# Moving the conditions of extra blocks ahead of the transposes, an earlier first expert, and an on-chip last sum, in a mixture-of-experts block

## The chip, the cores and the metric

The kernel runs on one core of a Trainium2 chip. The metric is the device time of one execution in microseconds (us), as the median of several runs. A difference under 1% (about 15 us here) can't be told from no change by a measurement of this kernel.

## The reference

The kernel computes one decoder block for 512 tokens of width 1024: an adaLN-modulated mixer (a state-space branch and a gated-MLP branch), then a top-4-of-32 mixture of experts, then a final norm. Almost all of the time goes into the experts:

```python
logits = (tok @ router_w + router_b)
top_val, top_idx = lax.top_k(logits, 4)
weights = softmax(top_val)
# for every expert e, on the rows that chose it:
gu = xb @ w_in[e] + b_in[e]             # 1024 -> 2048
gate, up = gu[:, :1024], gu[:, 1024:]
gate = jnp.minimum(gate, 7.0); up = jnp.clip(up, -7.0, 7.0)
act = (up + 1) * (gate * sigmoid(1.702 * gate))
y = act @ w_out[e] + b_out[e]           # 1024 -> 1024
out = out.at[row_tok].add(y * row_w)
# then
x = x + gate2 * out
return rms_norm(x, final_g)
```

All 32 experts are used, with float32 weights: 12 MB for each expert, 384 MB in all.

## The kernel before

The first 394 us compute the mixer, the router and the tables that say which token sits in which slot of which expert. Then come the 32 experts, one after the other, and at about 1508 us the final norm.

**Rows of an expert.** Each expert has a main block of 64 slots ("ab"). Its rows are gathered into `xab` by an indirect DMA that gpsimd issues, and the weights stream past them. An expert with more rows has extra blocks: a `single` (32 slots, "c") or a `pair` (64 slots), each inside a run-time condition `tc.If(single[e] > 0)` or `tc.If(pair[e] > 0)`. With the inputs of the runs shown, 15 of the 32 experts have one: twelve a single (experts 4, 6, 9, 12, 13, 16, 18, 22, 25, 27, 28, 30) and six a pair (11, 12, 17, 22, 26, 27). The other 17 are called plain below. The branch that skips a body on TensorE waits until the engine has finished what it has in hand.

**Weights.** `weight_loads` streams, for each expert, eight `wi` tiles and four `wo` tiles of 1 MB each through one pool of 19 buffers. SyncE (SP) issues the loads in order, in program order with its own copies of the conditions; a load can go out only when the readers of the buffer that it takes have let go of it. `prefetch(12 * (e + 3))` stands at the end of each expert.

**TensorE's order** is written out by hand (`manual_schedule`), as the code stands. For one expert: the two extra-block "up" products (`c_up`, and `ab_up` on the pair) inside their conditions; the main `ab_up` (64 matmuls in the trace's count, where each fp32 matmul instruction shows as two), with `before_last` called before its last four: it computes `swiglu` of the first half, transposes it (`act` to `aab`) and starts the second product with its biases. Then the conditions of the extra "down" products (`c_down`, pair `ab_out`); then the first half of the main "down" product (`ab_down`, 16), `halfway` (the second half's transposes, the next expert's row transposes `rows_of` and bias matmuls `main_sums`), and the second half (16). `give` scatters the result into the DRAM tensor `acc` by an indirect DMA with addition.

**The final norm** loads `acc` into four `fin` tiles of 128 x 1024, squares and sums on ScalarE, computes the inverse root by short VectorE steps (`final_rsqrt`), multiplies and stores. Two of the four tiles are multiplied by `final_g` on gpsimd.

**VectorE, ScalarE and gpsimd** are ordered by the framework's scheduler inside the experts, and by hand in the final norm.

## Time and profile before

| what | value |
|---|---|
| median of three runs | 1538.41 us (1537.32 to 1547.82) |
| profiled execution | 1535.88 us, span 1534.0 us |
| mean granted TensorE clock | 0.966 of full speed |
| TensorE matmul busy | 1392.9 us (91% of the span) |
| VectorE, ScalarE, gpsimd busy | 30%, 23%, 12% |
| DMA | 497.13 MB, mean 324 GB/s |

TensorE is busy most of the time and DMA is close to full in long stretches, so an average can't say which of the two sets the pace; each stretch has to be read by itself. The sum of busy time counts stretched matmuls too: TensorE at half its clock is busy twice as long.

### The profile page before, as it was taken

The page shows a single profiled execution, that of the slowest core. Times are in us where ns is not written, and L with a number is a line of the kernel's source. Part 1 is how long each engine was busy: PE and PEld are TensorE (multiplying, and loading weights), DVE is VectorE, ACT ScalarE, POOL GpSimd, SP SyncE. Part 2 cuts the span into 40 slices and gives each one's busy share as a digit, 9 for nine tenths or more (in the row PEclk, how much of TensorE's full clock was granted, in tenths as well). Part 3 has the DMA queues.
Part 4 walks back from the last instruction along what each step waited for, and adds up shares of the span by engine and source line. Part 5 has one row for each costly group of instructions (what it writes and reads, how often), then busy time and mean ns, then how long its engine had stood idle before and what let it go on. Part 6 is the DMA issues. An engine that isn't in the chain of part 4 may idle for free. (4 is left out here: it accounts for less than half of the span.)

```text
span 1534.0 us, 22365 instructions
## 1 busy us (share of the span) xinstructions
PE 1392.9 (91%) x7925; PEld 674.5 (44%) x7926; DVE 453.6 (30%) x1121; ACT 350.1 (23%) x841; POOL 187.1 (12%) x158
## 2 busy tenths in 40 slices
PE   5987999999699899979999999999999999999992
PEld 3766877787433233323333333333333333333330
DVE  7685842575421121111111211111112111121113
ACT  3453232334211111111120111111121121202112
POOL 3113000000201010201010110111101111101001
PEclk9998999999599999989999999999999999999997
DMA  9703687394799999999997899999999999769953
GB/s 312 205 14 120 195 290 237 117 388 149 290 399 400 410 405 409 404 401 404 410 402 276 326 399 407 407 354 397 406 403 384 391 411 406 296 231 356 403 215 132
DMA packets 128919, 497.13 MB, mean 324 GB/s; under 512 B 23588, under 2 KB 31236, under 8 KB 95972
## 3 DMA queue, kind: packets, MB, share of 16 engines
q1 hardware_dynamic: 113844, 468.50, 77.9%
q0 software_dynamic: 11888, 20.84, 5.9%
q10 hardware_dynamic: 3008, 5.38, 1.0%
q8 instruction: 116, 1.90, 0.5%
q14 instruction: 63, 0.52, 0.1%
HBM read 476.75 MB, written 20.40 MB: 324 GB/s over the span
## 5 line engine op out<-in xcount | busy, mean ns | idle before, releaser
L1313 PE MATMUL pu<-wi,xab 128*64 128x512 f32 x2048 | 458.7, 600 | 16.3 <-PEq L1432 13.5
L1313 PEld LDWEIGHTS pu<-wi,xab 128*64 128x64 f32 x2048 | 163.9, 138 | 288.2 <-issue 282.2
L1326 PE MATMUL pd<-wo,aab 128*64 128x512 f32 x1024 | 235.7, 602 | 22.5 <-PEq L1455 20.8
L1288 ACT ACTIVATE s<-g 128x256 f32<-128x256 f32 x88 | 36.7, 417 | 671.7 <-DVE g L1287 656.4
L1326 PEld LDWEIGHTS pd<-wo,aab 128*64 128x64 f32 x1024 | 74.1, 138 | 162.9 <-issue 148.9
L1287 DVE TENSOR_SCALAR g<-pu 128x256 f32<-128x256 f32 x64 | 27.0, 421 | 323.9 <-PE pu L1313 323.3
L1347 PE MATMUL pc<-wi,xc 128*32 128x512 f32 x768 | 88.4, 606 | 13.7 <-DMA wi<-in_moe_w_in 10.9
L1279 ACT ACTIVATE xab<-pt,sh2c,g2c 128x64 f32<-128x64 f32 x304 | 94.1, 415 | 11.4 <-PE pt L1273 9.7
L1313 PE MATMUL pc<-wi,xab 128*64 128x512 f32 x384 | 83.7, 594 | 1.2 <-ACT xab L1279 1.1
L1335 DVE SCALAR_TENSOR_TENSOR yab<-pd,tab,gate2h 128x512 f32<-128x512 f32 x32 | 24.0, 750 | 201.2 <-PE pd L1326 201.2
L1250 POOL DMA_INDIRECT xab<-hrow,tab x32 | 34.1, 1064 | 315.7 <-PE pt L1273 312.8
L1364 POOL DMA_INDIRECT acc<-yab,tab x32 | 51.0, 1594 | 151.8 <-DVE yab L1335 66.4
L386 PE MATMUL g<-hlo,whi 128*128 128x512 f32 x160 | 65.5, 410 | 2.8 <-DVE hlo L492 2.8
L386 PE MATMUL g<-hhi,whi 128*128 128x512 f32 x160 | 66.1, 413 | 1.7 <-ACT hhi L498 1.7
L386 PE MATMUL g<-hhi,wlo 128*128 128x512 f32 x160 | 64.7, 404 | 0.0
L1364 POOL DMA_INDIRECT acc<-yc,tab x12 | 19.9, 1656 | 361.4 <-DVEq L1455 242.2
L1287 DVE TENSOR_SCALAR g<-pc 128x256 f32<-128x256 f32 x24 | 10.2, 425 | 174.7 <-PE pc L1347 100.6
L174 ACT ACTIVATE whi<-wraw 128x1024 fp32r<-128x1024 f32 x46 | 47.4, 1054 | 57.5 <-PE g L386 36.0
L1281 ACT ACTIVATE aab<-pt 128x256 f32<-128x256 f32 x64 | 24.6, 384 | 150.3 <-PE pt L1273 150.3
L1347 PEld LDWEIGHTS pc<-wi,xc 128*32 128x32 f32 x768 | 23.3, 110 | 69.7 <-issue 52.4
L175 DVE TENSOR_TENSOR wlo<-wraw,whi 128x1024 fp32r<-128x1024 f32 x36 | 43.1, 1219 | 33.2 <-ACT whi L174 32.9
L1313 PEld LDWEIGHTS pc<-wi,xab 128*64 128x64 f32 x384 | 27.1, 137 | 55.2 <-issue 49.6
(446 smaller groups left out, 1589.2 us busy)
## 6 DMA issues: line engine op xcount, KB each, us to landing
wi<-in_moe_w_in SPq DMA_DIRECT2D x256, 1024.0 KB, 18.1
wo<-in_moe_w_out SPq DMA_DIRECT2D x128, 1024.0 KB, 19.8
adaw<-in_ada_w SPq DMA_DIRECT2D x16, 1024.0 KB, 8.3
wraw<-in_w_in SPq DMA_DIRECT2D x12, 1024.0 KB, 5.0
wraw<-in_ada_w SPq DMA_DIRECT2D x8, 1024.0 KB, 9.0
wraw<-in_w_out SPq DMA_DIRECT2D x4, 1024.0 KB, 4.9
xt<-in_x SPq DMA_DIRECT2D x4, 512.0 KB, 5.3
wraw<-in_w_in SPq DMA_DIRECT2D x4, 512.0 KB, 12.6
```

What stands on the lines that cost most here:

```text
L174: sc.activation(dst_hi, src, AF.Copy)
L175: lo.tensor_sub(dst_lo, src, dst_hi)
L386: pe.matmul(P["ps"][m], l, r, start=(k == 0 and n == 0), stop=(k == 2 * P["n"] - 1 and n == 2))
L1250: gp.indirect_dma_start(out=dst, out_offset=None, in_=rows_, in_offset=bass.IndirectOffsetOnAxis(ap=idx, axis=0), bounds_check=n * S - 1, ...
L1279: sc.activation(t[:, o:o + w], ps[:, o:o + w], AF.Identity, scale=g2c[:, k:k + 1], bias=sh2c[:, k:k + 1])
L1281: sc.activation(t, ps[:, 0:128 * n], AF.Copy)
L1287: v.tensor_scalar(g, p[:, 0:256], LIMIT, None, op0=OP.min)
L1288: sc.activation(sg, g, AF.Sigmoid, scale=ALPHA)
L1313: pe.matmul(p[u][64 * g:64 * g + 64, :].rearrange("p (a b) -> p a b", a=2), xT[:, k % 4, 64 * (k // 4):64 * (k // 4) + 64], wi[k][:, :, 51 ...
L1326: pe.matmul(p[64 * g:64 * g + 64, :], aT[:, k % 2, 16 * (k - k % 4):16 * (k - k % 4) + 64], wo[k // 2 + j][:, k % 2, 512 * g:512 * g + 512 ...
L1347: pe.matmul(p[32 * g:32 * g + 32, :].rearrange("p (a b) -> p a b", a=2), xT[:, k % 2, 32 * (k // 2):32 * (k // 2) + 32], wi[k][:, :, 256 * ...
L1364: gp.indirect_dma_start(out=rows_, out_offset=bass.IndirectOffsetOnAxis(ap=icol, axis=0), in_=y, in_offset=None, compute_op=OP.add)
```

## The change

Four edits, in the one diff:

1. The conditions move. `c_down` and the pair's "down" now stand in `before_last`, in front of the transposes of the first half. `c_up` and the pair's "up" become `extra_up`, and `halfway` of expert e calls `extra_up(e + 1)`, in front of the transposes of the second half: they run before the second half of expert e's own "down" product, and no condition with a body is left between two experts.
2. The first expert's "up" product begins early: half of its steps, `UP[:8]`, run before and behind the table matmuls, ahead of the condition `most > 6`.
3. The last expert's rows are not scattered to `acc`. `last_places` builds a one-hot matrix `hot` on VectorE, eight matmuls `ys` put the rows in token order, and VectorE adds them to `fin`, which is loaded from `acc` while the last expert still runs.
4. The final norm is written anew: three VectorE steps for each tile (two adds, one multiply by both factors), two inverse roots of two tiles each, and no gpsimd.

```diff
+    def sums(t, n, tile_):
+        r = tile_("slt")
+        sc.activation(r[0:n], t[0:n, 0:96], AF.Copy)
+        return r
+
+    def tables(r, n, reps, tab, mul, o, ps_, tile_):
...
+    UP = [(k, u) for k in range(4) for u in range(2)] + [(k, u) for u in range(2) for k in range(4, 8)]
+
+    def ab_up(xT, wi, p, between=None, steps_=UP):
+
+        for k, u in steps_:
             if between and (k, u) == (7, 1):
                 between()
...
-    def ab_out(pd, aT0, aT1, wo, row):
+    def ab_out(pd, aT0, aT1, wo, row, kept=False):
+
 
         ab_down(pd, aT0, 0, wo, (0, 1, 4, 5))
         aT1 = aT1()
         ab_down(pd, aT1, 1, wo, (0, 1, 4, 5))
         y = mo.tile([128, 512], F32, tag="yab", bufs=2, name="yab")
         v.scalar_tensor_tensor(y, pd, row[:, 2:3].bitcast(F32), gate2h, op0=OP.mult, op1=OP.mult)
+        if kept:
+            return y
         give(y, acc2, row[:, 1:2])
...
-    def later_tables(ch):
+    def later_sums(ch):
 
         t = PT()
         if ch > 1:
             later_hots(ch)
         for i in range(4):
             spread(t, 128, i)
-        s_ = rows_of(0) if ch == 1 else None
+        return sums(t, 128, mo_tile)
+
+    def later_tables(ch, r):
         tab = mo.tile([128, 512], F32, tag="yab", bufs=2, name="tl")[:, 0:384].bitcast(I32) if ch > 1 else None
         tab = tab.rearrange("p (n e w) -> p n e w", n=4, w=3) if ch > 1 else tab1
-        tables(t, 128, rep32, tab, 4.0, 0, PT, mo_tile)
+        tables(r, 128, rep32, tab, 4.0, 0, PT, mo_tile)
         if ch == 1:
-            tables(t, 64, rep64, tabp, 2.0, 2, PT, mo_tile)
+            tables(r, 64, rep64, tabp, 2.0, 2, PT, mo_tile)
             v.copy_predicated(tab1[:, 0], pair4.unsqueeze(2).to_broadcast([128, 32, 3]), tab1[:, 2])
         gp.dma_start(tabl[4 * ch - 2:4 * ch + 2].rearrange("n p f -> p n f"), tab.rearrange("p n e w -> p n (e w)"))
-        return s_
+
+    fin, places = [], {}
+
+    def load_fin():
+        for i in range(4):
+            nc.sync.dma_start(fin[i][:, 0], acc[128 * i:128 * i + 128])
+
+    def last_places(e):
+
+        hot = xab[(e + 1) % 3]
+        t = pos[:, 0:5]
+        v.tensor_copy(t[:, 4:5], tab0[:, 0, e, 1:2])
+        v.tensor_sub(t[:, 4:5], t[:, 4:5], offs[:, 2:3])
+        for i in range(4):
+            v.tensor_scalar(t[:, i:i + 1], t[:, 4:5], 0.5, -1.0 - 128.0 * i, op0=OP.mult, op1=OP.add)
+            v.tensor_scalar(hot[:, 128 * i:128 * i + 128], iota_l, t[:, i:i + 1], None, op0=OP.is_equal)
+        places["hot"] = hot
 
...
-    xT0 = later_tables(1)
+    slots1 = later_sums(1)
     sel0 = selectors(0)
+    p0 = main_sums(0, sel0)
+    xT0 = rows_of(0)
+    ab_up(xT0, W[0][0], p0, None, UP[:4])
+    later_tables(1, slots1)
+    ab_up(xT0, W[0][0], p0, None, UP[4:8])
     most = nc.values_load(nbt[0:1, 96:97], min_val=0, max_val=NBMAX)
     with tc.If(most > 6):
         for ch in (2, 3, 4):
-            later_tables(ch)
+            later_tables(ch, later_sums(ch))
         spaced(PT(), sel0, 62)
...
+    def extra_up(e, sel):
+
+        (wi, _), n, x_, last = W[e], e // 16, xce[e % 3], acts(3, "actc")
         with tc.If(single[e] > 0):
             c_up(transposed(x_[:, 512:768], 2, "xc", 2, True), wi, sel, n, last[2])
         with tc.If(pair[e] > 0):
@@ -1435,32 +1461,48 @@
             ab_up(xp, wi, up_biases(sel, n, pp))
             for t, a_ in zip(pp, last):
                 swiglu(t, a_)
+        return last
+
+    def expert(e, xT, sel, p, more=None):
+        (wi, wo), n = W[e], e // 16
+        x_ = xce[e % 3]
+        if e + 2 < NE:
+            gather_first(e + 2)
+            gather_more(e + 2)
+        sel1 = selectors(e + 1) if e + 1 < NE else None
+        act = acts(2, "act")
+        last = extra_up(0, sel) if e == 0 else more
         aT, nxt = [], []
 
         def before_last():
             swiglu(p[0], act[0])
+            with tc.If(single[e] > 0):
+                c_down(transposed(last[2], 2, "ac", 2), wo, sel, n, tab1[:, 0, e])
+            with tc.If(pair[e] > 0):
+                lT = [transposed(t, 2, "ac", 2) for t in last[0:2]]
+                ab_out(out_biases(spaced(PC(), sel, 5), sel, n), lT[0], lambda: lT[1], wo, tabp[:, 0, e])
             aT.append(transposed(act[0], 2, "aab", 2))
             aT.append(out_biases(pab.tile([128, 512], F32, tag="pd", name="pd"), sel, n))
 
         def halfway():
+            more_ = extra_up(e + 1, sel1) if sel1 is not None else None
             aT1 = transposed(act[1], 2, "aab", 2)
             if sel1 is not None:
-                nxt.extend((rows_of(e + 1), sel1, main_sums(e + 1, sel1)))
+                nxt.extend((rows_of(e + 1), sel1, main_sums(e + 1, sel1), more_))
             return aT1
 
-        ab_up(xT, wi, p, before_last)
+        ab_up(xT, wi, p, before_last, UP if e else UP[8:])
         swiglu(p[1], act[1])
-        with tc.If(single[e] > 0):
-            c_down(transposed(last[2], 2, "ac", 2), wo, sel, n, tab1[:, 0, e])
-        with tc.If(pair[e] > 0):
-            lT = [transposed(t, 2, "ac", 2) for t in last[0:2]]
-            ab_out(out_biases(spaced(PC(), sel, 5), sel, n), lT[0], lambda: lT[1], wo, tabp[:, 0, e])
-        ab_out(aT[1], aT[0], halfway, wo, tab0[:, 0, e])
+        if e == NE - 1:
+            last_places(e)
+            fin.extend(H([128, 2, 1024], name="fin") for _ in range(4))
+            load_fin()
+        places["y"] = ab_out(aT[1], aT[0], halfway, wo, tab0[:, 0, e], e == NE - 1)
         if e + 2 < NE:
             prefetch(12 * (e + 3))
         return nxt
 
-    s_ = xT0, sel0, main_sums(0, sel0)
+    s_ = xT0, sel0, p0
...
+        load_fin()
+
+    ys = []
+    for i in range(4):
+        ys.append([PC(), PC()] if i % 2 else [pab.tile([128, 512], F32, tag=f"pu{u}", name="ys") for u in range(2)])
+        for g in range(2):
+            pe.matmul(ys[i][g], places["hot"][64 * g:64 * g + 64, 128 * i:128 * i + 128],
+                      places["y"][64 * g:64 * g + 64], start=True, stop=True)
...
+    def final_add(i):
+        for g in range(2):
+            o = fin[i][:, 0, 512 * g:512 * g + 512]
+            v.tensor_add(o, ys[i][g], o)
+
+    def final_out(i):
+        v.scalar_tensor_tensor(fin[i][:, 1], fin[i][:, 0], fr[:, i:i + 1], fg, op0=OP.mult, op1=OP.mult)
 
     def final_store(i):
         nc.sync.dma_start(dap(out, i * 128 * 1024, [[1024, 128], [1, 1024]]), fin[i][:, 1])
 
+    r01, r23 = [final_rsqrt(slice(a, a + 2)) for a in (0, 2)]
+    for i in range(3):
+        final_add(i)
+        final_square(i)
+    for _ in r01:
+        pass
+    final_add(3)
+    final_square(3)
     for i in range(4):
-        final_square(i)
-    final_mul(0)
-    r0, r1_, r2 = [final_rsqrt(slice(a, b)) for a, b in ((0, 1), (1, 2), (2, 4))]
-    final_mul(2, gp)
-    final_mul(3, gp)
-    for _ in zip(range(4), r0):
-        pass
-    final_mul(1)
-    in_turn(chain(r0, (final_out(0, lo, lo + 256) for lo in range(0, 1024, 256))), r1_)
-    final_store(0)
-    final_out(1, eng=sc)
-    final_store(1)
-    for _ in r2:
-        pass
-    for i in (2, 3):
-        final_out(i, 0, 640)
-        final_out(i, 640, 1024, sc)
+        if i == 2:
+            for _ in r23:
+                pass
+        final_out(i)
         final_store(i)
```

On TensorE, around the first expert's start, from the slot sums (`pt<-rx,oh`) on; `slt,reps` are the table matmuls. Before:

```order
L1121 MATMUL pt<-rx,oh 128x96 x16
L1273 MATMUL pt<-ident,xab_3352 128x128 x4
L1201 MATMUL pt<-slt,reps 128x96 x5
L1410 TENSOR_LOAD nbt
L1411 COMPARE_AND_BRANCH
```

After:

```order
L1121 MATMUL pt<-rx,oh 128x96 x16
L1299 MATMUL pu<-bhl,sel 128x512 x2
L1276 MATMUL pt<-ident,xab_3352 128x128 x4
L1318 MATMUL pu<-wi,xab 64x512 x8
L1204 MATMUL pt<-slt,reps 128x96 x5
L1318 MATMUL pu<-wi,xab 64x512 x8
L1441 TENSOR_LOAD nbt
L1442 COMPARE_AND_BRANCH
```

The bias matmuls and half of the first expert's "up" product (`pu<-wi,xab`, 16 of 30 rows) now stand in front of the condition at `most > 6` (L1411 before, L1442 after), with the table matmuls between them.

On TensorE, from the first half of an expert's "down" product (`pd<-wo,aab`) to the conditions of the next expert's extra blocks. `xce` holds the extra blocks' rows, `pc` their sums. Before:

```order
L1326 MATMUL pd<-wo,aab 64x512 x8
L1273 MATMUL pt<-ident,act 128x128 x2
L1273 MATMUL pt<-ident,xab_3353 128x128 x4
L1296 MATMUL pu<-bhl,sel 128x512 x2
L1326 MATMUL pd<-wo,aab 64x512 x8
L1257 TENSOR_LOAD nbt x2
L1263 COMPARE_AND_BRANCH
L1263 UNCONDITIONAL_BRANCH x2
L1265 COMPARE_AND_BRANCH
L1265 UNCONDITIONAL_BRANCH x2
L1430 COMPARE_AND_BRANCH
L1273 MATMUL pt<-ident,xce_3356 128x128 x2
```

After, from the same first half on:

```order
L1331 MATMUL pd<-wo,aab 64x512 x8
L1456 COMPARE_AND_BRANCH
L1276 MATMUL pt<-ident,xce_3356 128x128 x2
L1299 MATMUL pc<-bhl,sel 128x512
L1355 MATMUL pc<-wi,xc 32x512 x32
L1456 UNCONDITIONAL_BRANCH x2
L1458 COMPARE_AND_BRANCH
L1276 MATMUL pt<-ident,xce_3356 128x128 x4
L1299 MATMUL pc<-bhl,sel 128x512 x2
L1318 MATMUL pc<-wi,xab 64x512 x32
L1458 UNCONDITIONAL_BRANCH x2
L1276 MATMUL pt<-ident,act 128x128 x2
```

What stood after the second half of `pd<-wo,aab` and the gather conditions now stands right behind the first half: the second half, the transposes of `act` and everything of the next main block come after both extra "up" products.

## Rows read from the trace of the kernel before

**Rows 1.** Groups by line, TensorE: busy us, mean ns, then idle before and releaser.

```profile
L1313 PE MATMUL pu<-wi,xab 128*64 128x512 f32 x2048 | 458.7, 600 | 16.3 <-PEq L1432 13.5 <-DMA wo<-in_moe_w_out 2.8
L1326 PE MATMUL pd<-wo,aab 128*64 128x512 f32 x1024 | 235.7, 602 | 22.5 <-PEq L1455 20.8 <-DMA wi<-in_moe_w_in 1.2 <-ACT aab L1281 0.5
L1347 PE MATMUL pc<-wi,xc 128*32 128x512 f32 x768 | 88.4, 606 | 13.7 <-DMA wi<-in_moe_w_in 10.9 <-ACT xc L1279 2.8
```

**Rows 2.** Windows of us: busy time by engine, PEclk, DMA share, GB/s.

```profile
620.00:690.00 70.00, 59.45 (x297) 21.37 (x293) 9.33 (x21) 11.68 (x37) 9.06 (x8) 0.94 1.03 402
760.00:850.00 90.00, 88.68 (x506) 33.37 (x504) 16.05 (x38) 16.16 (x49) 8.40 (x6) 1.00 0.87 335
1100.00:1200.00 100.00, 95.78 (x533) 35.89 (x531) 15.69 (x36) 17.95 (x55) 12.11 (x9) 1.00 1.00 394
```

**Rows 3.** TensorE in order of time, experts 1, 11 and 31: start, duration, work, [idle before].

```profile
439.85 13.10 PE L1313 MATMUL pu<-wi,xab 128*64 128x512 f32 x60 [0.72 <-PEq L1432]
...
455.51 3.65 PE L1326 MATMUL pd<-wo,aab 128*64 128x512 f32 x16 [0.94 <-PEq L1455]
...
464.75 1.51 PE L1313 MATMUL pu<-wi,xab 128*64 128x512 f32 x6 [0.73 <-PEq L1432]
...
745.46 0.63 PE L1273 MATMUL pt<-ident,xce 128*128 128x128 f32 x4 [0.65 <-PEq L1430]
...
1482.78 13.10 PE L1313 MATMUL pu<-wi,xab 128*64 128x512 f32 x60 [0.73 <-PEq L1432]
```

**Rows 4.** TensorE in order of time: main block of expert 4, singles of 9 and 22.

```profile
526.33 14.19 PE L1313 MATMUL pu<-wi,xab 128*64 128x512 f32 x60 [0.30 <-DMA wo<-in_moe_w_out]
...
689.02 1.93 PE L1347 MATMUL pc<-wi,xc 128*32 128x512 f32 x8 [2.41 <-DMA wi<-in_moe_w_in]
...
1139.80 1.06 PE L1347 MATMUL pc<-wi,xc 128*32 128x512 f32 x8 [0.95 <-DMA wi<-in_moe_w_in]
```

**Rows 5.** TensorE in order of time, the first expert.

```profile
405.34 1.47 PE L1201 MATMUL pt<-slt,reps 128*128 128x96 f32 x5 [2.62 <-ACT xab L1279]
409.71 1.22 PE L1296 MATMUL pu<-bhl,sel 128*128 128x512 f32 x2 [2.90 <-DVEq L1411]
412.49 14.79 PE L1313 MATMUL pu<-wi,xab 128*64 128x512 f32 x60 [1.56 <-PEq L1432]
```

**Rows 6.** SyncE's queue in order of time: a load of expert 1's weights.

```profile
406.93 0.33 SPq L946 DMA_DIRECT2D wi<-in_moe_w_in  x1
```

**Rows 7.** Windows of 4 us around the first expert, columns as in rows 2.

```profile
404.00:408.00 4.00, 1.47 (x5) 1.22 (x5) 1.50 (x7) 1.74 (x7) 1.36 (x2) 0.50 0.98 391
408.00:412.00 4.00, 1.22 (x2) 0.50 (x2) 0.64 (x5) 0.21 (x1) 0.84 (x1) 0.50 0.94 328
412.00:416.00 4.00, 3.51 (x10) 1.18 (x12) 0.00 (x0) 0.00 (x0) 0.00 (x0) 0.51 0.63 252
416.00:420.00 4.00, 4.00 (x22) 1.48 (x20) 0.00 (x0) 0.00 (x0) 0.00 (x0) 1.00 0.66 231
```

**Rows 8.** ScalarE in order of time, after expert 4's extra block.

```profile
526.59 0.42 ACT L1288 ACTIVATE s<-g 128x256 f32<-128x256 f32 x1 [10.19 <-DVE g L1287]
```

**Rows 9.** The chain that ended last, the tail: start, us, what.

```profile
1507.57 5.01 DMA acc<-yab,tab
...
1512.65 3.25 DMA fin<-acc
```

**Rows 10.** VectorE and ScalarE in order of time, the end of the final norm.

```profile
1526.03 0.15 DVE L1512 TENSOR_SCALAR fs<-fs 128x2 f32<-128x2 f32 x1
...
1528.06 0.16 DVE L1518 SCALAR_TENSOR_TENSOR fs<-fs 128x2 f32<-128x2 f32 x1
...
1528.83 0.60 ACT L1531 ACTIVATE fin<-fin,fs 128x384 f32<-128x384 f32 x1
```

**Rows 11.** Groups by line, VectorE, columns as in rows 1.

```profile
L1045 DVE TENSOR_TENSOR x<-g,x 128x512 f32<-128x512 f32 x8 | 5.5, 691 | 0.3
L1526 DVE TENSOR_TENSOR fin<-fin,fg 128x1024 f32<-128x1024 f32 x2 | 2.4, 1222 | 8.8 <-DMA fin<-acc 8.8
```

More of the change, by code (lines that the diff above doesn't have):

```diff
@@ L1193, in tile_hybrid_block @@
     pair4 = rt.tile([128, 32], mybir.dt.uint8, name="pair4")
-    def tables(t, n, reps, tab, mul, o, ps_, tile_):
+    def sums(t, n, tile_):
[3 more added lines that the diff above has]
+    def tables(r, n, reps, tab, mul, o, ps_, tile_):
         N = tab.shape[1]
-        r = tile_("slt")[0:n]
-        sc.activation(r, t[0:n, 0:96], AF.Copy)
         ps = ps_()
         for b, rep in enumerate(reps):
-            pe.matmul(ps[:, 96 * b:96 * b + 96], rep[0:n], r, start=True, stop=True)
+            pe.matmul(ps[:, 96 * b:96 * b + 96], rep[0:n], r[0:n], start=True, stop=True)
         pv = ps[:, 0:96 * N].rearrange("p (n v e) -> p n v e", n=N, v=3)
-        iv, em = [tile_(n).rearrange("p (n e) -> p n e", e=32)[:, 0:N] for n in ("iv", "em")]
+        iv, em = [tile_(m).rearrange("p (n e) -> p n e", e=32)[:, 0:N] for m in ("iv", "em")]
         v.tensor_scalar(em, pv[:, :, 0], 0.0, None, op0=OP.is_equal)
@@ L1213, in front_tile @@
         return sm.tile([128, 96], F32R, name=n) if n == "slt" else sm.tile([128, 64], F32, name=n)
-    tables(slot_ps, 64, rep64, tab0, 2.0, 2, M, front_tile)
+    tables(sums(slot_ps, 64, front_tile), 64, rep64, tab0, 2.0, 2, M, front_tile)
     cps = M()
@@ L1305, in up_biases @@
         return p
-    def ab_up(xT, wi, p, between=None):
-        for k, u in [(k, u) for k in range(4) for u in range(2)] + [(k, u) for u in range(2) for k in range(4, 8)]:
+    UP = [(k, u) for k in range(4) for u in range(2)] + [(k, u) for u in range(2) for k in range(4, 8)]
+    def ab_up(xT, wi, p, between=None, steps_=UP):
+        for k, u in steps_:
             if between and (k, u) == (7, 1):
@@ L1420, in tile_hybrid_block @@
     prefetch(24)
-    def expert(e, xT, sel, p):
-        (wi, wo), n = W[e], e // 16
-        x_ = xce[e % 3]
-        if e + 2 < NE:
-            gather_first(e + 2)
-            gather_more(e + 2)
-        sel1 = selectors(e + 1) if e + 1 < NE else None
-        act, last = acts(2, "act"), acts(3, "actc")
+    def extra_up(e, sel):
+        (wi, _), n, x_, last = W[e], e // 16, xce[e % 3], acts(3, "actc")
         with tc.If(single[e] > 0):
@@ L1505, in tile_hybrid_block @@
     fs, fr, ft, fu = [f16[:, n] for n in range(4)]
-    fin = [H([128, 2, 1024], name="fin") for _ in range(4)]
-    for i in range(4):
-        nc.sync.dma_start(fin[i][:, 0], acc[128 * i:128 * i + 128])
     def final_rsqrt(r):
@@ L1523, in final_square @@
         sc.activation(sq, fin[i][:, 0], AF.Square, scale=1.0 / 32.0, accum_out=fs[:, i:i + 1])
-    def final_mul(i, eng=v, lo=0, hi=1024):
-        eng.tensor_mul(fin[i][:, 1, lo:hi], fin[i][:, 0, lo:hi], fg[:, lo:hi])
-    def final_out(i, lo=0, hi=1024, eng=None):
-        o, r = fin[i][:, 1, lo:hi], fr[:, i:i + 1]
-        if eng is sc:
-            sc.activation(o, o, AF.Copy, scale=r)
-        else:
-            v.tensor_scalar(o, o, r, None, op0=OP.mult)
+    def final_add(i):
[4 more added lines that the diff above has]
+        v.scalar_tensor_tensor(fin[i][:, 1], fin[i][:, 0], fr[:, i:i + 1], fg, op0=OP.mult, op1=OP.mult)
     def final_store(i):
         nc.sync.dma_start(dap(out, i * 128 * 1024, [[1024, 128], [1, 1024]]), fin[i][:, 1])
-    for i in range(4):
-        final_square(i)
-    final_mul(0)
-    r0, r1_, r2 = [final_rsqrt(slice(a, b)) for a, b in ((0, 1), (1, 2), (2, 4))]
-    final_mul(2, gp)
-    final_mul(3, gp)
-    for _ in zip(range(4), r0):
-        pass
-    final_mul(1)
-    in_turn(chain(r0, (final_out(0, lo, lo + 256) for lo in range(0, 1024, 256))), r1_)
-    final_store(0)
-    final_out(1, eng=sc)
-    final_store(1)
-    for _ in r2:
-        pass
-    for i in (2, 3):
-        final_out(i, 0, 640)
-        final_out(i, 640, 1024, sc)
+    r01, r23 = [final_rsqrt(slice(a, a + 2)) for a in (0, 2)]
[6 more added lines that the diff above has]
+    final_square(3)
+    for i in range(4):
+        if i == 2:
+            for _ in r23:
+                pass
+        final_out(i)
         final_store(i)
```

## The prediction, as it was put on record

> **What bounds the kernel now.** I read the groups by line first, then the windows, then TensorE's row of work in order of time in four places, and last the chain that ended last.
>
> The groups [rows 1] show where TensorE stands still among the experts. Two of its idle times are conditions that skip an extra block: 13.5 us in front of the main "up" product and 20.8 us in front of the first half of "down". One is a wait for weights: 10.9 us in front of `c_up`. No single wait is large, so which one sets the pace has to come from the stretches.
>
> The windows [rows 2] answer that. From 620 to 690 the DMA share is 1.03 and the DMA engines move 402 GB/s; no stretch of this length shows much more, so the weight stream is full there, and the windows between 440 and 760 read alike. From 760 to 850 it is at 0.87 while TensorE works 88.7 of 90 us: there TensorE sets the pace and the buffers that it holds slow the stream. Near 1100 to 1200 the stream is at 1.00 again. So the kernel has a DMA-bound beginning (experts 4 to 9), and then a TensorE-bound rest with one more touch.
>
> TensorE's rows show the touches [rows 4]: `c_up` waits for its last `wi` tile, 2.41 us at expert 9 and 0.95 us at expert 22; experts 4 and 6 look like 9, and all four have a single. After expert 9's wait nothing in the beginning matters any more: TensorE starts that main block at a time that the weight's landing sets. What the change does ahead of 689 us therefore counts only by what it does to the landing at 689 us, and by how much work still follows it.
>
> A plain expert shows the unit prices [rows 3]: 60 matmuls take 13.10 us, 0.218 us each; from the end of the first half of "down" (455.51 + 3.65 = 459.16) to the end of the second half (464.75 - 0.73 = 464.02) it is 4.9 us; two skips cost 0.94 us ahead of "down" and 0.73 us ahead of "up". Expert 31 issues no gathers for a later expert, and its gap is 0.73 us too, so the loads and gather conditions at an expert's start cost nothing.
>
> **The change part by part, against the profiled 1535.9 us.**
>
> *Conditions moved, plain experts: 0.* Both double skips stay; they stand a few matmuls earlier. The engine still has to finish what it has in hand, and the transposes behind it did not wait before, so nothing is there for the skip to hide in. The bound is a gain of 0.94 - 0.5 or a loss of the like for each expert; I take 0.
>
> *Early need of weights: +4.9 us at expert 9, +4.9 us at expert 22.* `c_up(e+1)` now stands before the second half of "down" of expert e. Where it waits for a landing, the 4.9 us that used to be done before that wait now follow it. At expert 9 the landing at about 689 us is the stream's, not TensorE's, so the next main block starts 4.9 us later. At expert 22 TensorE waited 0.95 us already, hence the whole 4.9 us again, if the stream there keeps its place relative to TensorE: between 760 and 850 it was held up by TensorE [rows 2], so a TensorE that is late makes it late too. Bounds: 0 (the stream is early by then) to 4.9 at expert 22; 2.4 to 7 at expert 9. What is queued behind the waiting `c_up` on TensorE is the second half of "down", whose end lets go of two `wo` buffers; the pool has 19 buffers and an expert takes 12, so the stream still has others in hand, and I count no further delay.
>
> *First expert early: +3.7 us.* Before, TensorE reached the main "up" product of expert 0 at 412.49, after 2.90 us for VectorE and 1.56 us for the skips [rows 5]. After, the bias matmuls and the transposes come first; the row copies on ScalarE that kept the table matmuls waiting until 405.34 now gate the first steps, so these begin at about 404. That is 8 us earlier, and less the tables that now stand between, by itself it would bring the first main block's end forward by some 5 us. But the weights bind anyway from expert 4 on, so this gain is lost there. What isn't lost is the other side. Two loads of expert 1's weights, the first issued at 406.93 [rows 6], go out only when TensorE, for the second VectorE too, has passed the condition `most > 6`, and all that SyncE has to issue stands in line behind them. After, TensorE passes it only when 16 + 16 matmuls and the tables are done: 404.2 + 16 x 0.43 (the clock is 0.50 here [rows 7], twice the pitch of rows 3) + 1.5 for the tables [rows 5] + 16 x 0.218 comes to 416 with no rise of the clock in between, and to 413 or 414 with a rise that follows the steady work as it does after 412.49 [rows 5, 7]. I take 414. In the four windows from 404 to 420 [rows 7], 391, 328, 252 and 231 GB/s over 4 us each make 4.8 MB. After, I count full speed to 406, only gathers (0.3 MB) to 414.3, and full speed behind it (buffers of expert 0 come free together then): 0.8 + 0.3 + 2.3 = 3.4 MB, at most. The lack of 1.4 to 1.7 MB is 3.5 to 4.2 us at 402 GB/s: 3.7. Every landing of the full stretch moves by it, the one at expert 9 too. Bounds: 0 if the loads go out as before; 9.3 if the condition is passed only at 420.
>
> *Extra blocks' activation in the way: +3.3 us.* `swiglu` of an extra block now runs beside the second transposes of expert e. Its sigmoid on ScalarE (0.42 us [rows 8]) can stand in front of the copy of those transposes that TensorE waits for: about 0.3 us for each expert with an extra block. Six of the 15 lie between experts 10 and 21 and five or six behind, 11 x 0.3 = 3.3. Bounds 0 to 5.
>
> *Clock: +1 us.* After the wait at expert 4 the next 60 matmuls took 14.19 us instead of 13.10 [rows 3, 4]. The longer waits may cost that once more. Bounds 0 to 3. [...]
>
> *Tail: -6.5 us.* Before, y was ready at about 1507.3, then 5.01 us scatter, 3.25 us load and the norm [rows 9]; the last compute ended at 1528.83 + 0.60 = 1529.43 [rows 10], and the span ended 4.57 us later. After: 1507.3 + 0.9 (four matmuls of rows 3's pitch for the first tile's half sums) + 6 adds x 0.69 [rows 11] = 1512.3; an inverse root for two tiles takes 1528.06 + 0.16 - 1526.03 = 2.2 [rows 10], 1514.5; two adds, 1515.9; two multiplications at 1.22 (the nearest row is L1526's [rows 11]), 1518.3; root 2.2, 1520.5; two more, 1522.9; and 4.57 for the last store: 1527.5 against 1534.0. The load of `fin`, the one-hot and the jump over the spill code lie beside the last expert. Without that cover (the load waits for the scatter of expert 30, issued some 25 us earlier) it would cost 3.25 back. Bounds -3 to -7.
>
> *Sum:* 3.7 + 4.9 + 4.9 + 3.3 + 1 - 6.5 = +11.3, so 1547.2 in a profiled execution. The profiled one lay 2.5 us below the median of 1538.4, so I expect a median of **1549.5**.
>
> **The rivals.**
>
> *A, slower: the weight stream starts late.* The loads at the condition `most > 6` go out at 420 instead of 414, because the clock doesn't rise while TensorE works in pieces between the tables. Then the stream lacks 3.7 MB, 9.3 us instead of 3.7: 1549.5 + 5.6 = **1555**, and up to 1563 with the upper bounds of the clock and of the activations. It decides from a time of about 418 on. For it: the clock is 0.50 from 404 to 412 and 0.51 to 416, while TensorE works in pieces [rows 7]. Against it: after 412.49 it rose within 4 us.
>
> *B, only the tail counts.* The stream has slack at experts 9 and 22 that the trace doesn't show, since a late TensorE also takes buffers later: 1538.4 - 6.5 = **1532**. For it: the wait at expert 22 is only 0.95 us. Against it: a share of 1.03 in a whole window, 620 to 690 [rows 2], leaves nothing to give.
>
> *C, faster: a skip in front of transposes is cheap.* If only the branches remain and the draining of the engine vanishes in the transposes' own latency, each plain expert gains 0.94 + 0.73 less the branches. [...] Against it: at expert 11 one skip alone, in front of the transposes of a pair, left TensorE idle for 0.65 us [rows 3]. [...]
>
> *D, the change doesn't do what it says:* expert 0 doesn't begin early because its rows or weights aren't there. It changes nothing, for the gain is lost at expert 4 anyway; the stream's term stays.
>
> **How the numbers follow.** My forecast has 0.50 (its own range 1541 to 1558), A 0.20, B 0.17, C 0.13; D lies inside the first. The range 1529 to 1563 leaves out the lower two thirds of C and the top of A, some 0.15 together. One per cent is 15.4 us: slower by more than that is above 1553.8, two thirds of A and the upper third of my forecast, 0.30. Faster by more than that is below 1523, half of C: 0.07. The rest is 0.63.
>
> **What would show it.** In the profile after: the first 16 matmuls of expert 0 at about 404, and the load of SyncE that went out at 406.93 at about 414; DMA shares near zero between 408 and 414; waits of `c_up` for `wi` at experts 4, 6, 9 and 22 that are longer by about 5 us; the main block of expert 9 some 8 us later; double skips of 0.7 to 0.95 us that now stand in front of transposes; and from y to the end of the span some 20 us instead of 26.7 (1534.0 - 1507.3). The prediction is wrong if `c_up` waits no longer than before, if the idle time at skips falls below 0.4 us in plain experts, or if a new wait (for the copies on ScalarE, or of the last sum's matmuls) shows up in the groups.

## The result, and the profile after

The changed kernel takes 1548.9 us (median of 16 runs), the kernel before 1541.61 us (median of 16 runs beside them); the ratio is 1.0056, 95% interval 1.0044 to 1.0068. So it is slower by 0.56%, some 8.6 us (6.8 to 10.5), which lies inside the 1% named ahead, though the interval leaves out "no change". The forecast was 1549.5, 11.1 us over the 1538.4 of the kernel before; beside the changed kernel, the kernel before came out 3.2 us higher, at 1541.61. The two profiled executions have spans of 1546.0 and 1534.0 us, 12.0 us apart: the profiled one of the kernel before lies 5.7 us under its median, that of the changed kernel 1.3 us.

The groups by line of the changed kernel, TensorE, answer to [rows 1] (busy us, mean ns, then idle before and what ended it; L1318 is the "up" product, L1331 "down", L1355 `c_up`, L1276 the transposes):

```profile
L1318 PE MATMUL pu<-wi,xab 128*64 128x512 f32 x2048 | 457.9, 599 | 7.7 <-PEq L1458 5.3 <-issue 1.9 <-ACT xab L1282 0.5
L1331 PE MATMUL pd<-wo,aab 128*64 128x512 f32 x1024 | 234.0, 599 | 0.8 <-ACT aab L1284 0.5
L1355 PE MATMUL pc<-wi,xc 128*32 128x512 f32 x768 | 96.7, 637 | 24.2 <-DMA wi<-in_moe_w_in 20.9 <-ACT xc L1282 3.3
L1276 PE MATMUL pt<-ident,act 128*128 128x128 f32 x176 | 36.2, 293 | 39.7 <-PEq L1481 20.0 <-PEq L1458 18.3 <-PEq L1479 1.4
```

Two things are to be seen. The idle time at skips has changed its place and hardly its size: 13.5 + 20.8 us of it stood in front of "up" and "down" before (the rest of their 16.3 + 22.5 us were other waits, mostly for weights), 39.7 us stand in front of the transposes now, and 5.3 at the first expert, where TensorE stands still for 7.7 us in all. And `c_up` waits for weights for 20.9 us instead of 10.9.

TensorE in order of time in the changed kernel: a plain expert first, answering to [rows 3], then expert 9 and expert 22, answering to [rows 4] (start, duration, work, idle before).

```profile
444.81 5.75 PE L1318 MATMUL pu<-wi,xab 128*64 128x512 f32 x26
...
458.80 0.41 PE L1276 MATMUL pt<-ident,act 128*128 128x128 f32 x2 [0.94 <-PEq L1481]
...
464.82 0.41 PE L1276 MATMUL pt<-ident,act 128*128 128x128 f32 x2 [0.93 <-PEq L1458]
...
692.42 1.93 PE L1355 MATMUL pc<-wi,xc 128*32 128x512 f32 x8 [1.44 <-DMA wi<-in_moe_w_in]
694.67 0.66 PE L1276 MATMUL pt<-ident,act 128*128 128x128 f32 x2 [0.32 <-PEq L1458]
...
697.35 4.54 PE L1331 MATMUL pd<-wo,aab 128*64 128x512 f32 x16
701.72 13.04 PE L1318 MATMUL pu<-wi,xab 128*64 128x512 f32 x60
...
1154.04 1.06 PE L1355 MATMUL pc<-wi,xc 128*32 128x512 f32 x8 [0.67 <-DMA wi<-in_moe_w_in]
...
1175.19 5.32 PE L1318 MATMUL pu<-wi,xab 128*64 128x512 f32 x24
```

The main blocks of the same two experts before:

```profile
691.27 13.64 PE L1313 MATMUL pu<-wi,xab 128*64 128x512 f32 x60 [0.32 <-PEq L1432]
...
1155.99 13.04 PE L1313 MATMUL pu<-wi,xab 128*64 128x512 f32 x60
```

At expert 9 the last tile's products start at 692.42 instead of 689.02: the stream is 3.4 us late. The main block then starts 9.30 us behind them (701.72), where it started 2.25 us behind them before (691.27): 7.05 us more. 4.9 us of that is the second half of "down" with its transposes; the rest, 2.1 us, is that this work ran at a stretched pace after the waits (4.54 us for 16 matmuls that take 3.65 elsewhere). After a stretch in which `c_up` worked in pieces between landings, the granted clock was 0.54 from 692 to 696 and 0.60 from 696 to 700, close to the 0.50 of the window from 404 to 408 below, where it was 0.95 and 1.00 in the same windows before. At expert 22 the same distance grew from 16.19 to 21.15 us.

The windows of the changed kernel, answering to [rows 7] and [rows 2]:

```profile
404.00:408.00 4.00, 3.46 (x12) 1.47 (x12) 0.00 (x0) 2.48 (x8) 2.19 (x3) 0.50 1.00 415
408.00:412.00 4.00, 4.00 (x19) 1.55 (x17) 0.31 (x2) 0.00 (x0) 0.00 (x0) 0.87 0.15 52
412.00:416.00 4.00, 3.47 (x16) 0.88 (x14) 1.83 (x10) 0.57 (x2) 0.83 (x1) 1.00 0.19 53
416.00:420.00 4.00, 0.00 (x0) 0.00 (x0) 0.00 (x0) 0.00 (x0) 0.00 (x0) 0.91 0.88 274
620.00:690.00 70.00, 58.46 (x287) 18.77 (x287) 10.17 (x24) 10.84 (x33) 6.51 (x6) 0.95 1.02 406
```

From 408 to 416 the weight stream stands almost still (52 and 53 GB/s instead of 328 and 252). In the four windows from 404 to 420 it moves 3.2 MB instead of 4.8; at 402 GB/s the 1.6 MB that are lacking take 4.1 us. SyncE's queue shows why, answering to [rows 6], and TensorE's row of the first expert, answering to [rows 5], what became of the early start:

```profile
415.61 0.34 SPq L946 DMA_DIRECT2D wi<-in_moe_w_in  x1
```

```profile
405.86 5.21 PE L1318 MATMUL pu<-wi,xab 128*64 128x512 f32 x16 [0.55 <-ACT xab L1282]
411.00 0.89 PE L1204 MATMUL pt<-slt,reps 128*128 128x96 f32 x5
411.82 3.65 PE L1318 MATMUL pu<-wi,xab 128*64 128x512 f32 x16
420.76 2.79 PE L1318 MATMUL pu<-wi,xab 128*64 128x512 f32 x5 [5.28 <-PEq L1458]
```

The load that went out at 406.93 goes out at 415.61. The 32 early matmuls end at 415.5, but the conditions behind them take 5.28 us with nothing beside them, and expert 1 starts at 444.81 instead of 439.85.

The chain that ended last, in the changed kernel's tail, answers to [rows 9]:

```profile
1526.01 0.76 DVE yab L1341
...
1526.81 1.18 PE ys L1545 x4
...
1529.18 2.48 DVE fin L1575 x4
...
1535.16 2.39 DVE fin L1578 x2
...
1539.69 1.28 DVE fin L1578
```

No scatter and no load stand in it any more. From the end of y (1526.77) to the end of the span it is 19.2 us instead of 26.7.

### The profile page after: what moved, and what is told of

Same layout as the page of the kernel before. It is cut to its first block, busy times and chain, and to the rows that moved or that the text cites. A ratio compares the mean times of both kernels' runs of the same rounds, so it can differ in the third digit from the quotient of the medians.

```text
span 1546.0 us, 22408 instructions
## 1 busy us (share of the span) xinstructions
PE 1399.7 (91%) x7941; PEld 653.6 (42%) x7942; DVE 459.3 (30%) x1123; ACT 346.4 (22%) x837; POOL 181.2 (12%) x155
## 5 line engine op out<-in xcount | busy, mean ns | idle before, releaser
L1318 PE MATMUL pu<-wi,xab 128*64 128x512 f32 x2048 | 457.9, 599 | 7.7 <-PEq L1458 5.3
L1318 PEld LDWEIGHTS pu<-wi,xab 128*64 128x64 f32 x2048 | 144.8, 138 | 290.4 <-issue 284.4
L1331 PE MATMUL pd<-wo,aab 128*64 128x512 f32 x1024 | 234.0, 599 | 0.8 <-ACT aab L1284 0.5
L1331 PEld LDWEIGHTS pd<-wo,aab 128*64 128x64 f32 x1024 | 71.1, 138 | 142.7 <-issue 121.3
L1355 PE MATMUL pc<-wi,xc 128*32 128x512 f32 x768 | 96.7, 637 | 24.2 <-DMA wi<-in_moe_w_in 20.9
L1318 PE MATMUL pc<-wi,xab 128*64 128x512 f32 x384 | 83.7, 594 | 1.0 <-ACT xab L1282 0.9
L1276 PE MATMUL pt<-ident,act 128*128 128x128 f32 x176 | 36.2, 293 | 39.7 <-PEq L1481 20.0
L1276 PEld LDWEIGHTS pt<-ident,act 128*128 128x128 f32 x176 | 18.0, 142 | 105.6 <-issue 90.1
L1355 PEld LDWEIGHTS pc<-wi,xc 128*32 128x32 f32 x768 | 22.6, 112 | 89.5 <-issue 72.0
```

Source lines behind the costliest of these rows:

```text
L1276: pe.transpose(ps[:, 128 * j:128 * j + 128], src[:, 128 * j:128 * j + 128], ident)
L1318: pe.matmul(p[u][64 * g:64 * g + 64, :].rearrange("p (a b) -> p a b", a=2), xT[:, k % 4, 64 * (k // 4):64 * (k // 4) + 64], wi[k][:, :, 51 ...
L1331: pe.matmul(p[64 * g:64 * g + 64, :], aT[:, k % 2, 16 * (k - k % 4):16 * (k - k % 4) + 64], wo[k // 2 + j][:, k % 2, 512 * g:512 * g + 512 ...
L1355: pe.matmul(p[32 * g:32 * g + 32, :].rearrange("p (a b) -> p a b", a=2), xT[:, k % 2, 32 * (k // 2):32 * (k // 2) + 32], wi[k][:, :, 256 * ...
```

## The experiments

My theory: the up conditions' new place costs what follows a wait for weights, the early first expert costs a late stream, the tail gives back its share, the down conditions cost nothing. Rivals: the loss comes from the first expert alone, or from the conditions' places themselves. All runs have the changed tail, so **tail_only** is their base. Ratios are to the kernel before, with 95% intervals.

**tail_only.** From the changed kernel, conditions and first expert put back:

```diff
-        last = extra_up(0, sel) if e == 0 else more
+        last = extra_up(e, sel)
...
-            more_ = extra_up(e + 1, sel1) if sel1 is not None else None
...
         swiglu(p[1], act[1])
+        with tc.If(single[e] > 0):
+            c_down(transposed(last[2], 2, "ac", 2), wo, sel, n, tab1[:, 0, e])
...
-    ab_up(xT0, W[0][0], p0, None, UP[:4])
...
-        ab_up(xT, wi, p, before_last, UP if e else UP[8:])
+        ab_up(xT, wi, p, before_last, UP)
```

> The kernel before with the changed last sum and final norm alone: the conditions and the first expert stand as before. Both theories: only the tail's gain is left, which the two profiles put at 26.7 - 19.2 = 7.5 us, so about 1534 beside a kernel before at 1541.6. If the early load of the final tiles or the one-hot disturbs the last experts, less than 5 us are left.

Measured: 1534.49 us, ratio 0.997 [0.9954, 0.9987], so 4.6 us gained (2.0 to 7.1). Its profiled execution (span 1525.8) was the fastest of its seven; sizes are taken from the medians here.

**tail_up.** The same with the up conditions in `halfway`, as in the change.

> The changed last sum and norm, and the extra up products moved in front of the second half of the expert before (the down conditions and the first expert as before). My theory (the work that now follows a wait for weights costs 4.9 us at expert 9 and again at expert 22, a little at expert 16): 12 to 13 us over the run with the changed tail alone, about 1546. The rival that the whole loss comes from the late weight loads at the first expert: no loss here, about 1534.

Measured: 1552.49 us, ratio 1.0079 [1.0058, 1.01], 18 us over tail_only. The rival is out: the first expert stands as before here. But 18 (17 by the ratios) is more than 12 to 13. The trace shows a second cost:

```profile
442.12 0.43 PE L1276 MATMUL pt<-ident,act 128*128 128x128 f32 x2 [3.08 <-PEq L1460]
...
464.07 3.65 PE L1331 MATMUL pd<-wo,aab 128*64 128x512 f32 x16 [0.95 <-PEq L1495]
469.75 0.41 PE L1276 MATMUL pt<-ident,act 128*128 128x128 f32 x2 [2.02 <-PEq L1460]
```

The skip of the down conditions (L1495) costs 0.95 as ever; the skip of the up conditions, 3.65 us of matmuls later, costs 0.93 to 3.08 in front of the plain experts, most of them over 1.2. From expert 9 on the excess over 0.93 comes to 6 us, about what 18 has over 12.

**tail_down.** The same base with only the down conditions in `before_last`, as in the change; run twice.

> The changed last sum and norm, and the down conditions moved in front of the first transposes (nothing else). My theory: skips cost the same 0.9 us in the new place, and no wait for weights moves, so the same as the run with the changed tail alone, 1534, within 2 us. A rival that skips in front of transposes hide something: 0.3 to 0.5 us for each of 17 plain experts, 5 to 9 us less.

> The run with the down conditions and the tail once more, the same kernel: 9 us under the kernel before if the first result holds (ratio 0.9933), 5 us if it was on the lucky side.

Measured: 1529.9 us, ratio 0.9933 [0.9919, 0.9948], and 1530.64 us, ratio 0.9941 [0.9925, 0.9957]. The moved skip costs 0.92 to 0.98 us in the plain experts of both traces, so nothing hides in it; only at expert 8 it is longer, at the same place and nearly the same size in both:

```profile
662.19 0.66 PE L1276 MATMUL pt<-ident,act 128*128 128x128 f32 x2 [2.82 <-PEq L1483]
```

```profile
664.87 0.41 PE L1276 MATMUL pt<-ident,act 128*128 128x128 f32 x2 [2.88 <-PEq L1483]
```

The kernel before and tail_only have a long one there too (4.38 and 4.25 us); the wait for weights at expert 9 stands behind it, so it says nothing of the whole time. The medians lie 4 to 5 us under tail_only's: the first run's interval lies just under that of tail_only, the second's overlaps it. Where such a gain would come from I did not find: by their profiled executions tail_down is the slower one. That stays open. The two traces, of one kernel, also show how far a single trace can be trusted: the last landing of expert 9 lies 2.8 us apart in them (688.71 and 691.48). Of the versions that leave no work out it is the fastest, 9 us under the kernel before.

**tail_front.** The same base with only the early first expert.

> The changed last sum and norm, and the first expert's early up steps (conditions as before). My theory: the weight loads behind the condition go out 8 us later, the full stream is 3 to 4 us late at expert 9, and nothing follows it: 3 to 4 us over the run with the changed tail alone, about 1538. The rival that all of the loss of the changed kernel comes from here: 19 us over it, about 1553.

Measured: 1539.4 us, ratio 0.9998 [0.9985, 1.0011], 4.9 us over tail_only: my theory's side, not the rival's 1553. The early start is not just lost, it costs. How much is less sure: in its trace the last landing of expert 9 is 8.2 us later than before, not 3 to 4, and a long skip at expert 0 stands in the way besides:

```profile
441.41 5.34 PE L1331 MATMUL pd<-wo,aab 128*64 128x512 f32 x16 [4.81 <-PEq L1492]
```

**tail_up_down.** Both groups moved, the first expert as before.

> The changed kernel with the first expert put back as before: both groups of conditions moved, and the changed last sum and norm. The up move alone came out 18 us over the changed tail alone, and its profile shows the skip behind the first half of down at 1.2 to 3.1 us instead of 0.9, where another skip stands only those 16 matmuls ahead of it. My theory: with the down conditions moved too, more work lies between the two skips, both cost 0.9, and only the weights' early need is left: 10 to 13 us over the run with the down conditions alone (1530), about 1542. The rival that the up move costs its 18 us wherever the other skips stand: about 1548.

Measured: 1544.56 us, ratio 1.0034 [1.0018, 1.005]; 14 us over tail_down and 8 us under tail_up. Both skips cost 0.88 to 0.97 us again where both bodies are skipped:

```profile
L1276 PE MATMUL pt<-ident,act 128*128 128x128 f32 x176 | 35.9, 292 | 38.4 <-PEq L1483 19.0 <-PEq L1460 17.9 <-PEq L1481 1.5
```

That is 1 us above the 10 to 13 of the theory, and most of it stands where the theory has it: the trace is 4.5 us behind tail_down at expert 9's main block and 12.8 at expert 22's (1.7 and 12.2 behind the second run of tail_down, whose stream was late). Freed of how late the stream is, from expert 9's last landing to its main block it is 6.71 us here (688.76 to 695.47), and 2.26 in both runs of tail_down: 4.45 us more, with the work behind the wait at full pace (3.65 us for the 16 matmuls of "down").

**tail_up_behind.** From tail_up, the up conditions behind the second transposes and biases:

```diff
-            more_ = extra_up(e + 1, sel1) if sel1 is not None else None
             aT1 = transposed(act[1], 2, "aab", 2)
             if sel1 is not None:
-                nxt.extend((rows_of(e + 1), sel1, main_sums(e + 1, sel1), more_))
+                nxt.extend((rows_of(e + 1), sel1, main_sums(e + 1, sel1)))
+                nxt.append(extra_up(e + 1, sel1))
```

> As the run with the up move alone, but the extra up products stand behind the transposes and bias matmuls of the second half instead of in front of them. My theory: the skip lies 1.3 us of work farther from the one ahead of it and costs about 1 us again, and 3.7 us instead of 4.9 follow a wait for weights: about 1543. If the distance of the skips is not the cause, the skip stays at 1.2 to 3.1 us: about 1552 less 2.

Measured: 1553.77 us, ratio 1.0108 [1.0086, 1.0131]: 10 us more than I expected. The skips came out as expected; a new wait took the place:

```profile
L1331 PE MATMUL pd<-wo,aab 128*64 128x512 f32 x1024 | 235.2, 600 | 36.6 <-PEq L1495 17.1 <-ACT xab L1282 13.4 <-PEq L1460 4.9
L1355 PE MATMUL pc<-wi,xc 128*32 128x512 f32 x768 | 95.1, 634 | 34.1 <-ACT xc L1282 17.9 <-DMA wi<-in_moe_w_in 16.1
```

The up skip now lies in front of "down" (13.4 + 4.9 us over all experts, 0.9 each in a plain one; the 13.4 the trace puts down to ScalarE's row copies, which run at the same time). But `c_up` waits 17.9 us for ScalarE's copy `xc` instead of 2.8: the next main block's row copies (2.5 us) stand in front of it there. That the time came out near the 1550 of the other reading (the skip stays dear) is chance.

**extra_late.** The opposite: from tail_down, the up products in `before_last` of their own expert and the down products in `halfway`:

```diff
         def before_last():
             swiglu(p[0], act[0])
-            with tc.If(single[e] > 0):
...
+            late_.append(extra_up(e, sel))
...
         def halfway():
+            last = late_[0]
+            with tc.If(single[e] > 0):
...
             aT1 = transposed(act[1], 2, "aab", 2)
```

> The opposite move: the extra up products stand in the main up product ahead of its last four matmuls, in front of the first transposes, and the extra down products in front of the second transposes; last sum and norm as changed, first expert as before. My theory: where weights are late, the 13 us of the main block now run while they land and only the extra block's 6 to 7 us follow the last landing, so experts 9 and 22 end earlier by 4 to 7 us each: 1520 to 1526. The rival that the place of the conditions, not the weights, sets the cost: 1530 or, if the skips get dearer, 1540.

Measured: 1557.36 us, ratio 1.0107 [1.0086, 1.0128]: a clear miss. The main block now waits for weights itself:

```profile
L1318 PE MATMUL pu<-wi,xab 128*64 128x512 f32 x2048 | 475.7, 615 | 22.1 <-DMA wi<-in_moe_w_in 21.4 <-issue 0.6
```

That is not the whole of the loss: `c_up` waits for no weights at all any more (15.2 us in tail_down), but the main block's matmuls are busy 475.7 us instead of 457.6, at 615 ns instead of 599, and eight pauses at skips are 1.3 to 4.0 us long. That a landing is followed by less work did not help, because the landing itself came later: a condition that might read an expert's `wi` tiles now ends behind the main block, so a buffer that was let go of step by step during the main "up" product is held to its end, in plain experts too. I read this from the code and the late starts, no run isolates it.

**light_down, light_up_down, light_up.** To take the waits for weights away, every second `wi` load is left out, in tail_down, tail_up_down and tail_up:

```diff
+                if e > 1 and k % 2:
+                    W[e][0].append(W[e][0][-1])
+                    yield
+                    continue
                 t = H([128, 2, 1024], name="wi")
```

> The run with the down conditions and the tail, with a lighter weight stream: from expert 2 on, every second wi tile is not loaded, and its products use the tile before it (so 8 MB for each expert instead of 12; the products are those of other weights). All theories: no wait for weights is left, TensorE sets the pace, and the time is 10 to 25 us under that of the same kernel with the full stream, 1505 to 1520. It is the base for the next two.

> The same lighter stream (every second wi tile is not loaded and the one before it is used), with both groups of conditions moved. My theory, that the up move costs only by what follows a wait for weights: within 2 us of the lighter run with the down conditions alone. The rival that the up products in their new place cost by themselves (activations in the way, skips): 5 to 12 us more than it.

> The same lighter stream (every second wi tile is not loaded and the one before it is used), with the up conditions alone moved. If a skip that follows another one at 3.7 us is dear because the full stream slows what it needs, 0.9 us for each skip again and the time of the other two, within 3 us. If it is the distance of the skips alone, 1.2 to 3.1 us for each of 17 skips again and 8 to 25 us more.

Measured: 1513.87 us (0.9811 [0.9793, 0.983]), 1507.91 us (0.9786 [0.977, 0.9802]) and 1538.82 us (0.9985 [0.9967, 1.0003]). With the full stream the up move cost 14 us over tail_down; with the light one it gains 6, outside the 2 us that I expected. In the light runs' groups `c_up` waits for no weights at all:

```profile
L1359 PE MATMUL pc<-wi,xc 128*32 128x512 f32 x768 | 84.9, 594 | 2.8 <-ACT xc L1286 2.8
```

The gain of 6 us is not the move's. Two skips of light_down are long:

```profile
868.46 6.96 PE L1322 MATMUL pu<-wi,xab 128*64 128x512 f32 x20 [4.20 <-PEq L1464]
```

```profile
899.26 6.06 PE L1322 MATMUL pu<-wi,xab 128*64 128x512 f32 x16 [4.48 <-PEq L1464]
```

Main block by main block, light_down falls 11.9 us behind light_up_down from expert 13 to expert 16, at these two and the stretched work behind them. From expert 1 to 13, and again from 16 to 31, light_up_down loses only 0.9 and 1.0 us to it. So without waits for weights the move costs some 2 us, and some 12 of the 14 us are the weights', not the place's. Light_up shows the second cost alone: still 25 to 31 us dearer than the others, with up skips of 0.7 to 5.3 us. A full stream is no condition for dear skips (the DMA share was 0.80 from 500 to 700 and 0.66 from 700 to 900). Nor is the pause all that one costs: behind the skip of 2.23 us at 437 the 16 matmuls of "down" took 4.99 us instead of 3.65, at a granted clock of 0.72.

**tail_up_spaced.** From tail_up, four idle matmuls ahead of the up conditions:

```diff
+            if sel1 is not None:
+                idle = PC()
+                for _ in range(4):
+                    pe.matmul(idle, sel[:, 1], bhl[:, n, 0:512], start=True, stop=True)
             more_ = extra_up(e + 1, sel1) if sel1 is not None else None
```

> As the run with the up move alone, with four idle matmuls (1.4 us) of 128 x 512 added between the first half of down and the up conditions, 31 times, whose sums nobody reads. If the distance in time between the two skips is what makes the second dear, it costs 0.9 us in every plain expert, where it cost 1.2 to 3.1. If distance is not the cause, 1.2 to 3.1 us again. The whole time isn't a measure here: the added matmuls alone are some 43 us.

Measured: 1587.7 us. Twelve of sixteen plain up skips now cost 0.7 to 1.2 us, but four cost 2.1 to 4.9:

```profile
489.50 0.41 PE L1276 MATMUL pt<-ident,act 128*128 128x128 f32 x2 [1.07 <-PEq L1460]
...
1113.43 0.66 PE L1276 MATMUL pt<-ident,act 128*128 128x128 f32 x2 [4.92 <-PEq L1460]
```

So distance in time isn't the whole cause, and perhaps no cause: the added matmuls also shift all of the program behind them. The long skips at expert 8 and in light_down have 10 us of work and more between them and the skip ahead.

What the long ones have in common stands in the DMA records of the same traces. Each run has some 116 packets of 16 KB in a queue of the kind "instruction" (packets, MB, share of the engines' span; the kernel before):

```profile
q8 instruction: 116, 1.90, 0.5%
```

From 430 to 1505 us, the fourteen traces have 32 skips of over 1.7 us that end at TensorE's own sequencer (PEq). In all 32 such a packet begins within the pause or in the 1.6 us before it. Of the 402 skips of 0.6 to 1.25 us, 31 have one there. So a long skip goes together with a load of instructions. For which engine a packet was, the record doesn't say, and no run moves one by itself, so it is not shown to be the cause.

## Why the prediction was right

**Skips, 0: right.** 0.94 and 0.93 us in the new places where it was 0.94 and 0.73. In the plain experts that follow each other (1 to 3, and 18 to 21) the distance of the main blocks to those of before changes by only 0.1 us an expert. The 0.5 us in the bound for a gain was the author's estimate, and no run shows it: in the traces every pause at two skipped conditions in a row is at least 0.7 us.

**Early need of weights, +4.9 and +4.9: right, and low by what it left out.** Expert 9's main block came 10.45 us late: 3.4 by the stream, 4.9 by this term and 2.1 by the clock. Expert 22's came 19.2 us late, 7.3 more than expert 21's: 4.96 by this term and 2.3 by a stream that had fallen further behind. One of 2.0 us at expert 16 (its `c_up` waited too) had not been foreseen. The cause is shown by the pair of light runs, where without waits for weights the move costs some 2 us, and by the 4.45 us in tail_up_down. One sign failed: the wait of `c_up` grew by 2.7 us at expert 4, 4.0 at expert 9 and 3.9 at expert 22, not by 5, and at expert 6 it shrank by 1.9.

**First expert, +3.7: right in kind, near in size.** The load went out 8.7 us later, and the four windows from 404 to 420 lack 4.1 us of stream. At expert 9 it was 3.4 us in the trace, but two traces of one kernel differ by 2.8 there, and tail_front's has 8.2. By the ratios it was 0.28% (4.3 us) from tail_only to tail_front and 0.22% (3.4 us) from tail_up_down to the changed kernel, each uncertain by some 0.2 points. Two steps were wrong without weight. 404.2 + 16 x 0.43 + 1.5 + 16 x 0.218 = 416 was called the time without a rise of the clock, but its second 16 matmuls are at full clock already; without a rise it is 419.5. The clock did rise, to 0.87 from 408 to 412. And I had the first block end 5 us earlier; it ended 5 us later, because I counted the conditions behind `most > 6` as free where TensorE has nothing else in hand; they took 5.28 us.

**Extra blocks' activation, +3.3: wrong, it is near 0.** From expert 9 to 21 the distance to the kernel before went from 10.45 down to 9.5 and up to 11.91, 2.0 of it in the one step at expert 16, and behind expert 22 from 19.2 to 19.6. The sigmoid does stand right in front of the copy `aab`, as I had it:

```profile
694.93 0.42 ACT L1291 ACTIVATE s<-g 128x256 f32<-128x256 f32 x1 [18.63 <-DVE g L1290]
695.47 0.38 ACT L1284 ACTIVATE aab<-pt 128x256 f32<-128x256 f32 x1
```

What failed is that TensorE would wait for it: the row transposes and bias matmuls lie between, and in the whole program the "down" products of the main blocks wait 0.8 us (L1331 above).

**Clock, +1: low.** The work behind the wait at expert 9 took 2.1 us more than at full pace, at a granted clock of 0.54 and 0.60. `c_up` itself ran at 637 ns a matmul instead of 606. In size the 2.1 us lie between the 1 of the forecast and its upper bound of 3.

**Tail, -6.5: right.** -7.5 us by the two profiles (19.2 instead of 26.7 from y to the end), which is beyond the bound of -7. All twelve traces with this tail but that of extra_late have 19.2 or 19.3. The ratio of tail_only gives -4.6 (-2.0 to -7.1).

The sum: 10.45 + 1.5 + 7.3 + 0.4 - 7.5 = +12.1 by the profiles (12.0 between the spans), +11.3 forecast. The terms that were too small and the one that was too large made up for each other; that part is luck. So is how close 1549.5 came to 1548.9: the forecast was a loss of 11.1 us, and the measured loss is 8.6, with 10.5 as the upper end of its interval. By the ratios, taken one upon the other: the tail -0.30%, the down conditions about -0.33%, the up conditions about +0.97%, the early first expert +0.22%. Their sum is the measured +0.56% by construction, as each is the step from one version to the next. The forecast had the down conditions at 0, and by the profiles they are.

Of the rivals, A's late stream happened at the size of my forecast (415.61, not 420). B is out by the 14 us of the up move. C is out: no skip got cheaper. Its time rested on an estimate of what is left of two skips that no run shows; the runs have at least 0.7 us for two. D is out: expert 0 began at 405.86 instead of 412.49. The range's lower end, 1529, left out the whole of C, not two thirds of it.

## What to carry to other kernels

Work that needs a landing should not be moved ahead of work that doesn't, where the stream of weights is full (a DMA share of 1.02 from 620 to 690 here): what it jumped over then followed the wait, 4.9 us at expert 9 and 4.96 us at expert 22. A load that waited for an engine to pass a condition made what stood behind it in the issuing queue late (8.7 us here, with 52 and 53 GB/s from 408 to 416), so work put in front of such a condition was paid for in the stream (4.1 us). A saving at the end of the program (here the scatter and the load, 4.6 us by the ratio and 7.5 by the traces) was kept whole: it came out the same (19.2 or 19.3 us from y to the end) behind every order of the experts but that of extra_late, so it could be judged by itself. And where a step of the program is dear in one version and cheap in the next, a look at whether a load of instructions falls on it (32 of 32 long skips here, 31 of 402 short ones) comes before a theory of its place.

## What was not expected of the hardware

A skip of two conditions on TensorE cost 0.7 to 1.0 us nearly anywhere in these traces. Some took 1.2 to 5.3 us, even with a DMA share of 0.80 or 0.66 (light_up). Where 16 matmuls (3.65 us) lay between a skip and the one ahead of it, most were long: 1.2 to 3.1 us in tail_up. With 4.9 us of work between the two it was 0.9 to 1.0 us in the plain experts of tail_up_down and, behind its first expert (1.23), of the changed kernel; with 5 us of it, in another way, up to 1.2 us in twelve of sixteen. But long skips also came behind 10 us of work and more (4.20 and 4.48 us in light_down). What all 32 over 1.7 us between 430 and 1505 us share is a 16 KB load of instructions in the pause or just before it. The one at expert 8 came back in a second execution of the same kernel (2.82 and 2.88 us in tail_down), which speaks for the program and against chance. The 5.28 us at the first expert are of another kind: no such load begins in them or in the 1.6 us before.
